# First modulations from re-laid pages of w_ada with FFN products between them, weight pages requested ahead in a fixed order, and position tables added to the latents by accumulating transfers

## The chip, the cores and the metric

The kernel runs on one core of a Trainium2 chip. Its engines are TensorE (PE in the profile: matmuls; PEld is its weight load), VectorE (DVE), ScalarE (ACT), GpSimd (POOL) and SyncE (SP, whose queue issues most of the DMA transfers). The metric is the device time of one execution in microseconds (us). The kernel's time is the median of several runs.

## The reference

One layer of a backbone over 1024 latent tokens `x` and 256 context tokens `ctx`, with 1024 channels in fp32. What the change touches is its beginning:

```python
h = x + grid_pos_emb(rows)          # sin/cos of the row: channels 0-511; of the column: 512-1023
hc = ctx
mods   = split(silu(c) @ w_ada + b_ada, 9)       # w_ada: 1024 x 9216; nine vectors of 1024
mods_c = split(silu(c_ctx) @ w_ada + b_ada, 9)

def ffn_sublayer(h, shift, scale, gate, g, w_in, w_out):     # D_FF = 2816
    hn = rmsnorm(h, g) * (1 + scale) + shift
    a, b = split(hn @ w_in, 2)
    return h + 0.5 * gate * ((silu(a) * b) @ w_out)

h  = ffn_sublayer(h,  mods[0],   mods[1],   mods[2],   ...)
hc = ffn_sublayer(hc, mods_c[0], mods_c[1], mods_c[2], ...)
...   # projections, mLSTM, spatial gating, output projection, second FFN on the latents, final norm
```

## The kernel before, in words

Channels lie on the 128 partitions, in eight tiles `d`. The context is `hc[d]` (128 x 256), the latents are `h[tb][d]` (128 x 512) for two halves `tb` of the tokens. All products are made of three fp32r matmuls, since each operand is split into a high and a low part: `split` (L145, L146) writes the high part on ACT (a cast) and the low part on DVE (a subtraction).

**The head.** The first FFN on the context needs the modulations 0 (shift) and 1 (scale) for silu(c_ctx); the latents need the same two for silu(c) somewhat later. The first 2048 columns of `w_ada` (8.4 MB) are loaded in four quarters of two channel tiles each, 32 transfers of 256 KB with rows of 1 KB (`ada_page`, L845). For quarters 0, 1 and 3 PE multiplies two columns (silu(c), silu(c_ctx)) with the pages, 512 columns at a time, and gets rows (`ada_rows`, L851), which are copied out (`ada_copy`) and turned into columns by small matmuls (`ada_flip`). Quarter 2 is accumulated on DVE (`side`, L794) and reduced. `ada_done` and `ada_side` add the bias into `mods` and make `smod`; `mod0` then makes the modulated context `hnc[d]` as high and low part, two tiles at a time. `idle(n)` puts filler matmuls on PE (`junk`, L923). The order of PE, DVE and ACT up to the end of hidden feature tile f=0 is written out by hand (`manual_schedule`); behind it a scheduler sets each engine's order.

**The first product of the context's FFN.** `W` (`Weights`) streams 44 weight pages W0 to W43 of 512 KB, two for each of 22 feature tiles f. Each has a raw page (`raw`, loaded at L126) and a split page (`hl`, 3 buffers); a page is asked for when a split page may be taken, and SP's queue holds the requests in that order. `proj` (L182) makes 24 matmuls of 256 columns per page. Results go through ACT and DVE to `gc` and to DRAM (`gcsp`).

**The latents beside it.** At f = 1 to 8 the loop asks for the two tiles of `xT` of one channel tile (256 KB each). At f = 2 to 9 it queues, for the gaps of DVE and ACT, the position add (`add_pos`, L917, from a table `pos` of 128 x 320 in SBUF, 160 KB) and the square and sum of the norm (`Norm.sq`, L210). At f = 10 come the norm's sums on PE (`Norm.rstd`, L215), the broadcast (L231) and the normalisation in place. After the 44 pages PE goes on with the first product of the latents (`Stage`, L412).

**The output product of the latents' first FFN** (L536) runs through passes p of 11 weight pages each; `rw` are loads of w1o, `graw` of the gated features. In its second pass `base` reloads the latents from `xT` and adds the positions again (`add_pos` with a second copy of the table, `pos2`), since the residual is added there.

Of the kernel before, what the change touches and what calls it, by code (L numbers as in the profile page):

```python
# [23 lines left out]
NKT = D // 128  # L24
# [31 lines left out]
def _build(ctx, tc, nc, a, out):  # L56
# [50 lines left out]
    class Weights:  # L107


        def __init__(self, order, name):  # L110
            self.c = ExitStack()
            self.pool = self.c.enter_context(tc.tile_pool(name=name, bufs=1, reuse_waits="tile"))
            self.order = deque(order)
            self.ready = deque()
            self.held = 0
            self.n = 0

        def load(self):
            n, i, w = self.order.popleft()
            src = a[n][i]  # L120
            if self.n % 4 < 2:
                raw = self.pool.tile([128, w], F32, name="raw", tag="raw", bufs=2)
            else:
                raw = hnp.tile([128, w], F32, name="raw", tag="pg0" if self.n == 2 else "pg1", bufs=8)
            self.n += 1
            nc.sync.dma_start(raw, src)  # L126
# [12 lines left out]
        def done(self, n=1):  # L139
            self.held -= n  # L140
            while self.order and self.held < 3:
                self.load()
# [635 lines left out]
    cp.tile([128, 32], F32, name="pad")  # L778

    def ada_load(page, m, hf, k):  # L780
        pgt = page()
        o = m * 1024 + hf * 512
# [53 lines left out]
    NQ = 4  # L836
    QW = 1024 // NQ
    QD = QW // 128
    KP = 512 // QW

    def ada_page(qt, kp, tag):
        pg = hnp.tile([128, KP, 2, QW], F32, name="adapg", tag=tag, bufs=8)
        for i in range(KP):
            src = a["w_ada"][kp * KP + i].rearrange("p (m c) -> p m c", m=9)[:, 0:2, qt * QW:(qt + 1) * QW]
            nc.sync.dma_start(pg[:, i], src)  # L845
        return [pg[:, i].rearrange("p m c -> p (m c)") for i in range(KP)]

    def ada_rows(pr, pgs, kp):
        for i, pg in enumerate(pgs):
            k = kp * KP + i  # L850
            T.matmul(pr[0:2, 0:2 * QW], sc2[:, :, k], pg, start=k == 0, stop=k == NKT - 1, skip_group_check=True)  # L851

    def ada_copy(pr):
        row = t2("adrow", shape=(2, 2 * QW))
        S.copy(row, pr[0:2, 0:2 * QW])
        return row

    def ada_flip(pc, row):
        for j in range(2 * QD):
            T.matmul(pc[:, 2 * j:2 * j + 2], row[:, j * 128:(j + 1) * 128], ident[0:2, 0:2], start=True, stop=True,  # L860
                     skip_group_check=True)

    def ada_side(qt, reds):
        bv = vs_("b_ada").rearrange("p (m d) -> p m d", m=9)
        cs = slice(qt * QD, (qt + 1) * QD)
        p8 = sm_ps("p8")
        for q, red in enumerate(reds):
            T.matmul(p8[:, q * 16:q * 16 + 16], grp4, red[:, 0:16], start=True, stop=True)
        for q in (1, 0):
            for r in range(4):  # L870
                sl = slice(32 * r, 32 * r + 32)
                V.tensor_add(mods[sl, 0:2, q, cs],
                             p8[sl, q * 16:q * 16 + 16].rearrange("p (m d r) -> p m d r", m=2, r=4)[:, :, :, r], bv[sl, 0:2, cs])
            scale_mod(0, 1, q, "g_ffn1", cs)

    def ada_done(qt, pc):
        sl = slice(qt * QD, (qt + 1) * QD)
        bv = vs_("b_ada").rearrange("p (m d) -> p m d", m=9)
        for q in (1, 0):
            V.tensor_add(mods[:, 0:2, q, sl],  # L880
                         pc[:, 0:4 * QD].rearrange("p (m d q) -> p m d q", m=2, q=2)[:, :, :, q], bv[:, 0:2, sl])
            done = scale_mod(0, 1, q, "g_ffn1", sl)
        return done
# [20 lines left out]
    pos = fxpage("pos", F32, (128, 320))  # L904

    def load_c(hcp, n):
        for i, pg in enumerate(hcp):
            nc.sync.dma_start(pg, a["cT"][i * n:(i + 1) * n].rearrange("d p t -> p d t"))

    def add_pos(tb, d, h=h, pos=pos):  # L910
        hv = h[tb][d].rearrange("p (r c) -> p r c", c=64)
        if d < 4:
            pv = pos[:, d * 16 + tb * 8:d * 16 + tb * 8 + 8].unsqueeze(2).to_broadcast([128, 8, 64])
        else:
            o = 64 + (d - 4) * 64
            pv = pos[:, o:o + 64].unsqueeze(1).to_broadcast([128, 8, 64])
        V.tensor_tensor(hv, hv, pv, ALU.add)  # L917
# [11 lines left out]
    def mod0(*ds):  # L929
        ts = [t2("nt")[:, 0:256] for _ in ds]  # L930
        for d, t in zip(ds, ts):
            S.activation(t, hc[d], AF.Identity, bias=mods[:, 0, 1, d:d + 1], scale=smod[:, 0, 1, d:d + 1])
            S.copy(hnc[d][:, 0, :], t)
        for d, t in zip(ds, ts):
            (V if d % 2 else G).tensor_tensor(hnc[d][:, 1, :], t, hnc[d][:, 0, :].bitcast(F32), ALU.subtract)

    def scaled0():
        for d in range(NKT):
            V.tensor_tensor(hc[d], hc[d], nct.rb, ALU.mult)
# [3 lines left out]
    sides = [t2("adacc") for _ in range(2)]  # L943

    def side(kp, pgs):
        for i, pg in enumerate(pgs):
            for q in range(2):
                ada_acc(V, sides[q], pg, q, kp * KP + i, kp + i == 0)

    load_c(hcp, 4)  # L950
    pgs = {}
    for qt, kp in ((2, 0), (0, 0), (0, 1), (2, 1), (0, 2), (0, 3), (2, 2), (1, 0), (1, 1), (2, 3), (1, 2), (1, 3),
                   (3, 0), (3, 1), (3, 2), (3, 3)):
        pgs[qt, kp] = ada_page(qt, kp, "pg1" if qt % 2 else "pg0")
    idle(30)
    for d in range(NKT):
        nct.sq(d)
    side(0, pgs[2, 0])
    prs = {0: mm_ps("adr")}
    ada_rows(prs[0], pgs[0, 0], 0)  # L960
    nct.rstd()
    ada_rows(prs[0], pgs[0, 1], 1)
    idle(3)
    side(1, pgs[2, 1])
    ada_rows(prs[0], pgs[0, 2], 2)
    nct.bcast()
    ada_rows(prs[0], pgs[0, 3], 3)
    row = ada_copy(prs[0])
    scaled0()
    side(2, pgs[2, 2])  # L970
    idle(4)
    pc = sm_ps("adc")
    ada_flip(pc, row)
    ada_done(0, pc)
    mod0(0, 1)
    prs[1] = mm_ps("adr")
    for kp in range(NKT // KP):
        ada_rows(prs[1], pgs[1, kp], kp)
    row = ada_copy(prs[1])
    side(3, pgs[2, 3])  # L980
    reds = [cp.tile([128, 32], F32, name="adred", tag="adred", bufs=2) for _ in range(2)]
    for acc, red in zip(sides, reds):
        ada_red(acc, red, 0)
    prs[3] = mm_ps("adr")
    ada_rows(prs[3], pgs[3, 0], 0)
    pc = sm_ps("adc")
    ada_flip(pc, row)
    ada_done(1, pc)
    mod0(2, 3)
    ada_rows(prs[3], pgs[3, 1], 1)  # L990
    ada_side(2, reds)
    for kp in (2, 3):
        ada_rows(prs[3], pgs[3, kp], kp)
    W.load()
    mod0(4, 5)
    row = ada_copy(prs[3])
    W.load()

    def last0():
        pc = sm_ps("adc")  # L1000
        ada_flip(pc, row)
        ada_done(3, pc)
        mod0(6, 7)
        W.load()

    nc.sync.dma_start(pos, a["pos"])
# [10 lines left out]
    for f in range(NF):  # L1017
        if 0 < f <= NKT:
            for tb in range(2):
                nc.sync.dma_start(h[tb][f - 1], a["xT"][f - 1, :, tb * 512:(tb + 1) * 512])  # L1020
        if 2 <= f < 2 + NKT:
            for tb in range(2):
                slow(add_pos, tb, f - 2)
                slow(n1[tb].sq, f - 2)
# [9 lines left out]
        if f > 12:  # L1034
            A.preload()
        wa = W.take("w1i", 2 * f)
        wb = W.take("w1i", 2 * f + 1)
        if f % 2 == 0:
            pa, pb = mm_ps("pa"), mm_ps("pb")
        for ks in (range(6), (6, 7)) if f == 0 else (range(NKT),):  # L1040
            for pt, w_ in ((pa, wa), (pb, wb)):
                proj(pt[:, f % 2 * 256:f % 2 * 256 + 256], w_, hnc, f % 2 == 0 and ks[0] == 0, ks)
                if f == 0 and ks[0] == 0 and pt is pa:
                    last0()
                if ks[-1] == NKT - 1:
                    W.done()
        if f == 0:
            order.close()
# [88 lines left out]
    pos2 = A.rg.tile([128, 512], F32, name="ft", tag="ft", bufs=1)[:, 0:320]  # L1137
    nc.sync.dma_start(pos2, a["pos"])

    def base(hv, tb, d):  # L1140
        return (lambda: nc.sync.dma_start(hv[tb][d], a["xT"][d, :, tb * 512:(tb + 1) * 512]),
                lambda: add_pos(tb, d, hv, pos2))
# [13 lines left out]
    load_c(hcp, 2)  # L1156
# [1172 lines left out]
def layout(x, c, ctx, c_ctx, w_ada, b_ada, g_ffn1, w_ffn1_in, w_ffn1_out, g_mix, w_in, b_gates,  # L2329
# [15 lines left out]
    r["cT"] = np.ascontiguousarray(ctx.T).reshape(8, 128, 256)  # L2345
# [61 lines left out]
```

## Time and profile before

| what | value |
|---|---|
| runs | 2642.66, 2642.14, 2639.4 us, median 2642.14 us |
| profiled execution | 2639.9 us, of which the span of the instructions is 2638.1 us |
| granted TensorE clock, mean | 0.997 |
| busy | PE 99%, PEld 84%, DVE 75%, ACT 46%, POOL 3% of the span |
| transfers | 448.5 MB, mean 170 GB/s |
| chain that ended last | PE 93%, DVE 2%, issue 2%, DMA 2%, ACT 1% |

Busy is the time in which an engine has an instruction under way; for PE that includes fillers. The chain that ended last is followed back from the last instruction, at each step to what released it. The DMA figures are a mean over stages of very different load, so the stages have to be read one by one.

### The profile page before, as it was taken

Reading aid. Unit: us, or ns where it says so; the run is one execution under the profiler, and the core shown is the slowest. Engines: PE = TensorE matmul, PEld = TensorE weight load, DVE = VectorE, ACT = ScalarE, POOL = GpSimd, SP = SyncE. Lnnn points to the kernel's source line nnn. Section 1 sums busy time; section 2 is a strip of 40 time slices with the busy share of each in tenths; the row PEclk is TensorE's granted clock in tenths of the full one; section 3 lists DMA queues with packets and bytes.
Section 4 is the critical chain, followed back from the end, with each engine's and each line's share of the span. In section 5 each row is a group of like instructions: output and inputs, shape, how many; then the busy total and the mean of one; then the engine's idle time right before and its main releaser. Section 6 shows DMA issues by size and latency. Waiting matters only on the chain.

```text
span 2638.1 us, 35899 instructions
## 1 busy us (share of the span) xinstructions
PE 2621.8 (99%) x12856; PEld 2205.1 (84%) x12856; DVE 1978.8 (75%) x3546; ACT 1205.6 (46%) x2175; POOL 75.8 (3%) x158
## 2 busy tenths in 40 slices
PE   9999999999999999999999999999999999999998
PEld 6998888888889878888888888888887888888887
DVE  7988688687989646777765878778799766665855
ACT  5664344444347525564443454333346444344433
POOL 0000000000000000000000002221000000000000
PEclk9999999999999999999999999999999999999999
DMA  9833344368587222346653566546341333337644
GB/s 312 311 113 127 128 164 161 117 224 307 169 283 268 77 80 85 111 162 205 196 172 112 166 206 247 180 150 206 125 157 39 128 136 123 113 125 282 199 159 177
DMA packets 200083, 448.54 MB, mean 170 GB/s; under 512 B 20192, under 2 KB 54496, under 8 KB 199904
## 3 DMA queue, kind: packets, MB, share of 16 engines
q1 hardware_dynamic: 199472, 445.85, 49.6%
q8 instruction: 101, 1.65, 0.3%
q14 instruction: 78, 0.64, 0.1%
q10 hardware_dynamic: 432, 0.39, 0.0%
HBM read 324.92 MB, written 121.32 MB: 169 GB/s over the span
## 4 chain that ended last, share of the span: by engine, by line
PE 93%; DVE 2%; issue 2%; DMA 2%; ACT 1%; SPq 0%; POOL 0%; POOLq 0%; ACTq 0%; DVEq 0%
PE qa L412 18%; PE pq L1380 17%; PE po L536 13%; PE qb L412 13%; PE pt L1864 6%; PE pr L1299 6%; PE po L2239 3%; PE pa L182 2%; PE pc L1166 2%; PE pb L182 2%; PE pn L2024 2%; PE pu L1700 1%; PE pn L2022 1%; PE pkc L1359 1%; PE pvc L1456 1%
## 5 line engine op out<-in xcount | busy, mean ns | idle before, releaser
L146 DVE TENSOR_TENSOR ring<-rawq,ring 128x512 fp32r<-128x512 f32 x408 | 281.3, 690 | 221.2 <-ACT ring L145 218.5
L536 PE MATMUL po<-gring,wring 128*128 128x512 f32 (+1 forms) x1896 | 424.0, 384 | 0.1
L536 PEld LDWEIGHTS po<-gring,wring 128*128 128x128 f32 x1896 | 349.4, 188 | 70.8 <-ACT px L693 0.9
L145 ACT CAST ring<-rawq 128x512 fp32r<-128x512 f32 x408 | 253.4, 622 | 309.2 <-PE pq L1380 86.1
L412 PE MATMUL qa<-fc,ring 128*128 128x512 f32 x1056 | 252.3, 389 | 0.0
L412 PEld LDWEIGHTS qa<-fc,ring 128*128 128x128 f32 x1056 | 198.2, 188 | 41.4 <-DVE fc L146 0.4
L1380 PE MATMUL pq<-fc,ring 128*128 128x512 f32 x864 | 207.3, 392 | 0.0
L145 ACT CAST wring<-rw 128x512 fp32r<-128x512 f32 x154 | 95.7, 622 | 216.6 <-PE po L536 184.7
L1380 PEld LDWEIGHTS pq<-fc,ring 128*128 128x128 f32 x864 | 161.4, 188 | 33.0
L1864 PE MATMUL pt<-yp,ring 128*128 128x512 f32 x768 | 184.4, 394 | 0.0
L1864 PEld LDWEIGHTS pt<-yp,ring 128*128 128x128 f32 x768 | 143.0, 188 | 28.2
L146 DVE TENSOR_TENSOR wring<-rw,wring 128x512 fp32r<-128x512 f32 x154 | 105.6, 686 | 80.7 <-ACT wring L145 80.5
L1380 PE MATMUL pq<-fa,ring 128*128 128x512 f32 x576 | 141.9, 394 | 0.0
L1380 PE MATMUL pq<-fb,ring 128*128 128x512 f32 x576 | 136.8, 391 | 0.0
L412 PE MATMUL qa<-fa,ring 128*128 128x512 f32 x528 | 129.6, 395 | 3.5 <-DVE ring L146 3.5
L412 PE MATMUL qa<-fb,ring 128*128 128x512 f32 x528 | 126.8, 390 | 0.0
L412 PE MATMUL qb<-fb,ring 128*128 128x512 f32 x528 | 126.6, 389 | 0.0
L1380 PEld LDWEIGHTS pq<-fb,ring 128*128 128x128 f32 x576 | 107.5, 188 | 22.4 <-issue 0.2
L412 PE MATMUL qb<-fc,ring 128*128 128x512 f32 x528 | 126.2, 389 | 0.0
L412 PE MATMUL qb<-fa,ring 128*128 128x512 f32 x528 | 126.2, 389 | 0.0
L1380 PEld LDWEIGHTS pq<-fa,ring 128*128 128x128 f32 x576 | 106.9, 188 | 21.9 <-DVE ring L146 0.2
L794 DVE SCALAR_TENSOR_TENSOR adacc<-adapg,sc,adacc 128x512 f32<-128x512 f32 x154 | 111.8, 747 | 17.8 <-DMA adapg<-in_w_ada_dram 17.0
(380 smaller groups left out, 4671.5 us busy)
## 6 DMA issues: line engine op xcount, KB each, us to landing
adapg<-in_w_ada_dram SPq DMA_DIRECT2D x144, 256.0 KB, 3.7
fsp<-fhl SPq DMA_DIRECT2D x66, 512.0 KB, 2.7
gring<-fsp SPq DMA_DIRECT2D x66, 512.0 KB, 4.3
raw<-in_w1i_dram SPq DMA_DIRECT2D x44, 512.0 KB, 5.4
graw<-fsp SPq DMA_DIRECT2D x88, 256.0 KB, 3.2
rawq<-in_w1i_dram SPq DMA_DIRECT2D x38, 512.0 KB, 3.7
rawq<-in_w2i_dram SPq DMA_DIRECT2D x38, 512.0 KB, 3.4
fsp<-p SPq DMA_DIRECT2D x66, 256.0 KB, 2.1
```

The costliest lines, as they stand in the source:

```text
L145: hi = S.copy(hl[:, 0, :], src)
L146: return hi, V.tensor_sub(hl[:, 1, :], src, hl[:, 0, :].bitcast(F32))
L182: T.matmul(pt, x, y, start=first and i == 0, stop=i == n - 1, skip_group_check=True)
L412: T.matmul(pt, hl[:, x, sl], pages[p][k][:, y, :], start=first and i == 0, stop=i == 11, skip_group_check=not first)
L536: T.matmul(pt[:, cs], w[:, x, sl], g[:, y, cs], start=grp and kp == 0 and i == 0, stop=kp == NFP - 1 and i == 2, skip_group_check=not grp)
L794: eng.scalar_tensor_tensor(acc, pgt, sc2[:, q, k:k + 1], acc, ALU.mult, ALU.add)
L1166: T.matmul(pt, hl[d // 4][:, x, sl], g[:, y, :], start=f == 0 and d % 2 == 0 and i == 0, stop=f == NF - 1 and i == 2, skip_group_check=True)
L1299: T.matmul(self.pt[m], pg[:, x, sl], hl[:, y, :], start=first and k == 0 and i == 0, stop=k == 3 and i == 2, skip_group_check=not first)
L1380: T.matmul(pt, hl[:, x, k * 128:(k + 1) * 128], pg[k][:, y, :], start=first and k == 0 and i == 0, stop=k == 3 and i == 2, skip_group_chec ...
L1864: T.matmul(pt, hl[:, x, k * 128:(k + 1) * 128], pg[:, y, :], start=kh + k + i == 0, stop=kh == 1 and k == 3 and i == 2)
L2024: T.matmul(pn[:, 0:257], qi[:, c_, :], self.C[d][:, c_, :], start=False, stop=c_ == 1)
L2239: T.matmul(pt, hl[:, x, k * 128:(k + 1) * 128], FO[p][k][:, y, :], start=first and k == 0 and i == 0, stop=k == 3 and i == 2, skip_group_c ...
```

## The change

1. `w_ada`'s first 2048 columns are re-laid on the host into 16 units (m, d) of 512 KB, each one channel tile d of modulation m, with rows of 4 KB. Eleven units (`UNITS`) are used as stationary operand on PE, 8 fp32 matmuls each (L949), and give columns for both conditioning vectors at once. Five units (`SIDE`), transposed, go to DVE: one fused multiply and reduction per conditioning vector against the vector spread over all partitions (`scB`). `spread` makes that on PE for the context; the latents' one is a broadcast load. The latents' five reductions are queued at f = 2 to 6.
2. The matmuls of f=0 and f=1 (`first`) stand between the units, channel tile by channel tile, as `mod0` delivers them. Order by hand now ends behind f=1. Fillers: 16 instead of 30 + 3 + 4.
3. Units, context halves and weight pages are requested in one written order. `W` fetches raw pages as soon as a raw buffer is to be had, up to eight ahead of the split, with five split pages instead of three; requests for `xT` and for the next stage are kept behind the last weight page asked for (`issue_after`).
4. `add_pos` no longer runs on DVE: the tables are expanded on the host to `posx` (8 x 128 x 1024), and a transfer on the GpSimd queue adds 256 KB from DRAM to each latent tile, 16 in the first product's stage and 16 in the output product's. The two loads of the small table go.

```diff
 class Weights:
-        def load(self):
+        def fetch(self):
             n, i, w = self.order.popleft()
             src = a[n][i]
             if self.n % 4 < 2:
                 raw = self.pool.tile([128, w], F32, name="raw", tag="raw", bufs=2)
             else:
-                raw = hnp.tile([128, w], F32, name="raw", tag="pg0" if self.n == 2 else "pg1", bufs=8)
+                raw = hnp.tile([128, w], F32, name="raw", tag="pg1", bufs=8)
             self.n += 1
-            nc.sync.dma_start(raw, src)
-            hl = self.pool.tile([128, 2, w], F32R, name="hl", tag="hl", bufs=3)
+            with ExitStack() as es:
+                if self.asked is not None:
+                    es.enter_context(tc.issue_after(self.asked.ins))
+                self.asked = nc.sync.dma_start(raw, src)
+            self.raws.append((n, i, w, raw))
+
+        def load(self):
+            if not self.raws:
+                self.fetch()
+            n, i, w, raw = self.raws.popleft()
+            hl = self.pool.tile([128, 2, w], F32R, name="hl", tag="hl", bufs=5)
             split(hl, raw)
             self.ready.append((n, i, hl))
             self.held += 1
+            if self.order:
+                self.fetch()
...
-    def add_pos(tb, d, h=h, pos=pos):
...
-        V.tensor_tensor(hv, hv, pv, ALU.add)
+    def add_pos(tb, d, h=h):
+        G.dma_start(h[tb][d], a["posx"][d, :, tb * 512:(tb + 1) * 512], accum_op=ALU.add)
...
+    for u in ("hc0", (1, 0), "hc1", (1, 1), (0, 0), (1, 2), (0, 1), (1, 3), (0, 2), "W", (0, 3), (1, 4), "W", (0, 4), (1, 5),
+              (0, 5), "W", (1, 6), (0, 6), "W", (1, 7), (0, 7), "W", "W", "W", "W"):
+        if u == "W":
+            W.fetch()
+        elif u in ("hc0", "hc1"):
+            load_c(hcp, 4, int(u[2]))
+        else:
+            fetch_unit(*u)
...
+    def side(m, d, q):
+        V.tensor_tensor_reduce(waste, page[m, d], scB[q], 1.0, vs_("b_ada")[:, m * 8 + d:m * 8 + d + 1], ALU.mult, ALU.add,
+                               mods[:, m, q, d:d + 1])
...
+    def unit(m, d):
...
+        for k in range(NKT):
+            T.matmul(pc[:, c:c + 128].rearrange("p (r q) -> p r q", q=2), page[m, d][:, k * 128:(k + 1) * 128],
+                     sc2[:, :, k].unsqueeze(1).to_broadcast([128, 64, 2]), start=k == 0, stop=k == NKT - 1,
+                     skip_group_check=True)
...
-    for f in range(NF):
-        if 0 < f <= NKT:
+    for f in range(1, NF):
+        if f <= NKT:
+            with tc.issue_after(W.asked.ins):
+                for tb in range(2):
+                    nc.sync.dma_start(h[tb][f - 1], a["xT"][f - 1, :, tb * 512:(tb + 1) * 512])
             for tb in range(2):
-                nc.sync.dma_start(h[tb][f - 1], a["xT"][f - 1, :, tb * 512:(tb + 1) * 512])
+                add_pos(tb, f - 1)
         if 2 <= f < 2 + NKT:
+            if f - 2 < len(SIDE):
+                slow(side, *SIDE[f - 2], 0)
             for tb in range(2):
-                slow(add_pos, tb, f - 2)
                 slow(n1[tb].sq, f - 2)
```

PE's order in the head before, from the last row products to the second weight page (`adr`, `p8`, `adc`: modulations; `pa`, `pb`: products of f=0; the number behind a name is the tile's own):

```order
L851 MATMUL adr_347<-adapg_181,sc2_98 2x512 x2
L868 MATMUL p8_369<-adred_339,cst_86 128x16
L868 MATMUL p8_369<-adred_340,cst_86 128x16
L851 MATMUL adr_347<-adapg_184,sc2_98 2x512 x2
L851 MATMUL adr_347<-adapg_187,sc2_98 2x512 x2
L182 MATMUL pa_408<-hnc_132,hl_388 128x256 x6
L182 MATMUL pa_408<-hnc_133,hl_388 128x256 x6
L182 MATMUL pa_408<-hnc_134,hl_388 128x256 x6
L860 MATMUL adc_428<-cst_86,adrow_399 128x2 x4
L182 MATMUL pb_409<-hnc_132,hl_403 128x256 x6
```

And now, from the eighth unit to the ninth and tenth (L949 with `adaU` is a unit, L195 is the line of `proj`):

```order
L949 MATMUL adc_354<-sc2_98,adaU_161 128x128 x8
L195 MATMUL pa_372<-hnc_131,hl_309 128x256 x6
L949 MATMUL adc_380<-sc2_98,adaU_167 128x128 x8
L195 MATMUL pa_372<-hnc_132,hl_309 128x256 x3
L195 MATMUL pb_373<-hnc_131,hl_349 128x256 x6
L195 MATMUL pb_373<-hnc_132,hl_349 128x256 x3
L949 MATMUL adc_413<-sc2_98,adaU_173 128x128 x8
L195 MATMUL pa_372<-hnc_132,hl_309 128x256 x3
```

The products moved in front of the last units; behind the last of the eleven (`adaU_179`) 60 matmuls of f=0 and f=1 are left.

SP's queue before, where the last pair of latent tiles is asked for (`raw` is a weight page, `raw_985` W18, `h` a latent tile; the waits are on semaphores of earlier transfers and on engines):

```order
L126 DMA raw_952<-in_w1i_dram 128x1024 [waits DMAHW1_49,DVE_49]
L1064 DMA gcsp_105<-gc_846 128x512 [waits DMAHW2_49,Activation_49]
L1064 DMA gcsp_105<-gc_847 128x512 [waits DMAHW3_49,DVE_49]
L126 DMA raw_985<-in_w1i_dram 128x1024 [waits DMAHW4_49,PE_49]
L1020 DMA h_119<-in_xT_dram 128x512 [waits DMAHW5_49]
L1020 DMA h_127<-in_xT_dram 128x512 [waits DMAHW6_49]
L126 DMA raw_1031<-in_w1i_dram 128x1024 [waits DMAHW7_49]
```

And now the same place (`raw_999` is W28, `raw_970` W27):

```order
L131 DMA raw_970<-in_w1i_dram 128x1024 [waits DMAHW6_49]
L1121 DMA gcsp_105<-gc_1004 128x512 [waits DMAHW7_49,Activation_49]
L131 DMA raw_999<-in_w1i_dram 128x1024 [waits DMAHW0_49,DVE_49]
L1121 DMA gcsp_105<-gc_1005 128x512 [waits DMAHW1_49,DVE_49]
L1078 DMA h_119<-in_xT_dram 128x512 [waits DMAHW2_49]
L1078 DMA h_127<-in_xT_dram 128x512 [waits DMAHW3_49]
L131 DMA raw_1049<-in_w1i_dram 128x1024 [waits DMAHW4_49,DVE_49]
```

The last pair stood behind W18 and now stands behind W28; the first two pairs stand behind W16. W28's raw buffer was W24's, which DVE must have split, into the split page that PE's use of W19 makes free.

PE's order at the latents' norm sums before (`p4`; `pa_1144` and `pb_1145` are f=10, whose pages are W20 and W21):

```order
L182 MATMUL pb_1002<-hnc_135,hl_1033 128x256 x6
L182 MATMUL pa_1144<-hnc_132,hl_1066 128x256 x6
L215 MATMUL p4_1152<-ones_88,acc_583 128x1 x4
L182 MATMUL pa_1144<-hnc_133,hl_1066 128x256 x6
L182 MATMUL pa_1144<-hnc_134,hl_1066 128x256 x6
L215 MATMUL p4_1193<-ones_88,acc_615 128x1 x4
L182 MATMUL pa_1144<-hnc_135,hl_1066 128x256 x6
```

And now (`pb_1154` ends f=11 with page W23; `pa_1358` is f=12):

```order
L195 MATMUL pb_1154<-hnc_133,hl_1110 128x256 x6
L195 MATMUL pb_1154<-hnc_134,hl_1110 128x256 x6
L228 MATMUL p4_1161<-ones_88,acc_591 128x1 x4
L195 MATMUL pa_1358<-hnc_131,hl_1139 128x256 x4
L228 MATMUL p4_1202<-ones_88,acc_610 128x1 x4
L195 MATMUL pa_1358<-hnc_131,hl_1139 128x256 x2
```

The sums moved from the start of f=10 (16 pages behind the end of f=1) to the start of f=12 (20 pages).

More of the change, by code (lines that the diff above doesn't have):

```diff
@@ L834, in ada_steps @@
             yield
[L836 to L883, printed above, removed]
+    SIDE = ((0, 0), (0, 4), (0, 5), (0, 6), (0, 7))
+    UNITS = ((1, 0), (1, 1), (1, 2), (0, 1), (1, 3), (0, 2), (0, 3), (1, 4), (1, 5), (1, 6), (1, 7))
+    BANK = {0: 0, 1: 0, 2: 1, 3: 1, 4: 2, 5: 3, 6: 4, 7: 5}
     smod = cp.tile([128, 3, 2, 8], F32, name="smod")
@@ L950, in _build @@
[L950 to L960, printed above, removed]
+    V.tensor_scalar(bias1, vs_("b_ada")[:, 8:16], 1.0, None, ALU.add)
+    idle(16)
@@ L961, in _build @@
+    unit(1, 1)
+    side(0, 0, 1)
+    unit_done(1, 0)
     nct.rstd()
[L962 to L965, printed above, removed]
+    unit(1, 2)
+    unit(0, 1)
     nct.bcast()
[L967 to L978, printed above, removed]
```

233 lines of the change are left out of this document (160 added, 73 removed).

## Prediction

> **What bounds the kernel now.** I read the page's table of engines first, then the chain of waits of the first 60 us, then the windows and the DMA view of the stages that the diff touches.
>
> ```profile
> PE 2621.8 (99%) x12856; PEld 2205.1 (84%) x12856; DVE 1978.8 (75%) x3546; ACT 1205.6 (46%) x2175; POOL 75.8 (3%) x158
> ```
>
> TensorE (PE) is busy in 99% of the span, but a busy PE is not always PE at useful work. In the head the chain of waits shows what it does:
>
> ```profile
> 0.99 9.07 PE junk L923 x60
> 36.09 1.24 DVE hl L146
> 37.38 2.18 PE pa L182 x16
> ...
> 45.67 2.64 PE pa L182 x22
> 48.31 2.64 PE pb L182 x22
> 50.95 2.88 PE pa L182 x24
> ```
>
> Columns: start, length, what. PE starts with 30 filler matmuls (60 records, 9.07 us) and begins the first FFN product at about 37 us. Hidden features f=0 and f=1 are done at 50.95; I call this point T0. From there a weight page is 24 matmuls in 2.88 us (0.12 us each), one after the other. What the head waits for is the load:
>
> ```profile
> GB/s 0 163 231 377 352 348 352 348 348 349 349 348 349 356 335 350 348 349 349 348 391 394 399 408 150 98 324 408 382 307 359 232 180 213 315 255 363 262 310 359
> adapg<-in_w_ada_dram SPq DMA_DIRECT2D x32, 256.0 KB, 6.1
> h<-in_xT_dram SPq DMA_DIRECT2D x9, 256.0 KB, 5.5
> ```
>
> This is the DMA view of 0 to 60 us, in slices of 1.5 us. The 32 loads of w_ada (8.4 MB, rows of 1 KB) run at 348 GB/s; the W pages behind them (30 to 36 us, rows of 4 KB) at 391 to 408.
>
> After T0 both the transfers and PE are close to full. Three windows, one row of the timeline, SP's waits of 0 to 170 us, and the rows of the position adds:
>
> ```profile
> 60.00:70.00 10.00, 10.00 (x86) 10.00 (x85) 8.86 (x12) 6.95 (x10) 0.00 (x0) 1.00 0.93 320
> 90.00:100.00 10.00, 10.00 (x87) 10.00 (x85) 7.55 (x12) 5.59 (x8) 0.00 (x0) 1.00 0.96 317
> 106.00:168.00 62.00, 62.00 (x516) 61.83 (x515) 59.38 (x81) 47.22 (x69) 0.00 (x0) 1.00 0.59 208
> 97.59 0.95 PE L215 MATMUL p<-ones,acc 128*128 128x1 f32 x8
> SPq L126 <- DVE hl L146: 55.6, 20, 6.4
> L917 DVE TENSOR_TENSOR h<-h,pos x16: 682/685/695, 43.4 to 85.4; 128x512 f32<-128x512 f32 x16
> L917 DVE TENSOR_TENSOR h<-h,ft x16: 682/685/694, 620.9 to 654.4; 128x512 f32<-128x512 f32 x16
> ```
>
> The windows give PE, PEld, DVE, ACT and POOL busy time, granted clock, DMA share and GB/s. DMA is 93 to 96% busy up to the latents' norm sums on PE (row of 97.59); after them VectorE (DVE) is, 59.38 of 62. SP's queue waits 55.6 us in the first 170 for splits of weights (L126 behind DVE), so a transfer queued behind a weight page goes out late. The two L917 rows are the 32 position adds.
>
> The adds' second stage is the FFN's output product near 620 us. Windows, then the DMA view of 620 to 640, a row of the chain and two of the timeline:
>
> ```profile
> 610.00:620.00 10.00, 10.00 (x46) 8.07 (x46) 6.30 (x16) 6.21 (x12) 0.00 (x0) 1.00 0.98 324
> 620.00:630.00 10.00, 9.86 (x43) 7.79 (x42) 6.36 (x10) 3.72 (x7) 0.00 (x0) 1.00 0.98 356
> 630.00:640.00 10.00, 10.00 (x45) 8.28 (x45) 7.07 (x11) 4.64 (x8) 0.00 (x0) 1.00 1.00 370
> DMA packets 3076, 7.27 MB, mean 363 GB/s; under 512 B 340, under 2 KB 340, under 8 KB 3075
> q1 hardware_dynamic: 3075, 7.25, 98.3%
> rw<-in_w1o_dram SPq DMA_DIRECT2D x6, 512.0 KB, 6.3
> h<-in_xT_dram SPq DMA_DIRECT2D x9, 256.0 KB, 6.3
> 609.55 7.56 DMA rw<-in_w1o_dram
> 588.51 1.75 PE L536 MATMUL po<-gring,wring 128*128 128x512 f32 x7
> 637.64 0.69 DVE L146 TENSOR_TENSOR wring<-rw,wring 128x512 fp32r<-128x512 f32 x1 [0.50 <-ACT wring L145]
> ```
>
> The transfers stand at 98 to 100%, and the chain already runs through a load of w1o at 609.55. Of the second pass, page 8's split is done at 637.64+0.69 = 638.3. PE started the product at 588.51 and takes 12 matmuls of about 10/44 us, 2.72 us, per page; the window of 620 lacks two or three of them (0.5 us). Page 8, after 11 pages of the first pass and 8 of the second, is due at 588.5+19x2.72+0.5 = 640.7. The slack is 2.4 us.
>
> **The change part by part.**
>
> Head. Out go 21 of 37 fillers, the row products, their copies, flips and DVE reductions; in come 8 spreading matmuls, 11 units of 8 matmuls on PE and five reductions on DVE. A row with 128x128 fp32 matmuls only, two records each:
>
> ```profile
> 6.00:8.00 2.00, 2.00 (x20) 2.00 (x19) 1.19 (x3) 1.86 (x7) 0.00 (x0) 1.00 1.05 346
> ```
>
> That is 0.2 us a matmul, so 1.6 us a unit. On PE: fillers to about 6 us, spreading 1.6, units 17.6, norm and broadcast about 1.5, then 60 products of 0.12 us behind the last unit: 34 us, earlier than the loads allow. The loads up to the last unit are 0.1 (vec), 0.13 (cst), 1.05 (hc), 8.4 (16 units) and 2.1 MB (four W pages): 11.8 MB. All have rows of 4 KB now, except small ones, so I take the rate of the W pages, about 400 GB/s: 29.5 us from about 2 us, plus 2 for the tail of a landing, 33.7. Then one unit (1.6) and 60 x 0.12 = 7.2: T0 = 42.5, a gain of 8.5. At 348 GB/s the load ends 4.4 us later and the gain is about 4; if the last transfers overlap more it is 9.5. I take 8.5, since the rows of 4 KB are the nearest.
>
> Position adds in the FFN's first product. Off DVE go 16 x 0.685 = 11 us, worth nothing here: PE ends every step to 97 us, and the five extra reductions for the latents (about 1.2 each by the row of 128x1024 below) come in. In come 16 transfers of 256 KB on the GpSimd queue, each behind its xT load. POOL is idle in the windows above, so nothing queues behind them there but each other. They land on the DMA. On PE, the norm sums now stand 20 pages behind T0 (the order rows above), 20 x 2.88 = 57.6; before, 16 pages. By then the DMA must bring W9 to W28 (20 pages, 10.5 MB; the five split pages and the raw buffers hold those up to W8), xT (4.2), 8 gcsp (2.1) and the added pages (4.2): 21.0 MB in 57.6 us, 365 GB/s. The rows above had 317 to 320 at a share of 0.93 to 0.96, and the best full stretch 363. There is no slack.
>
> Latency bounds it from below. The last xT pair stands behind W28 on SP, whose buffer is free when PE is done with W19 (16 pages after W3: T0+46.1) and W24 is split. A cast, the groups of splits and of sums on DVE, and the page's row of w_ada's loads:
>
> ```profile
> 44.06 1.06 ACT hl L145
> L146 DVE TENSOR_TENSOR hl<-raw,hl 128x1024 fp32r<-128x1024 f32 x38 | 46.4, 1220 | 3.6 <-ACT hl L145 3.5
> L210 DVE TENSOR_TENSOR acc<-acc,sq 128x512 f32<-128x512 f32 x14 | 9.0, 683 | 0.0
> adapg<-in_w_ada_dram SPq DMA_DIRECT2D x144, 256.0 KB, 3.7
> ```
>
> T0+46.1+1.06+1.22 = T0+48.4; xT 5.5; the adding transfer, if it is like a load, 5.5; square and sum about 1.4: T0+60.8, so PE stalls 3.2. With the quiet 3.7 for both: T0+57.2, no stall. From above: an addition in SBUF must read what it adds to. If each added byte costs two, 25.2 MB at 363 GB/s take 69.4 us, and with 1.4 behind it the stall is 13.2. I take the middle of 3.2 and 13.2, 8.2, for want of any row of such a transfer. The Trainium skill, "Collectives: The Full Stack", section "The bandwidth ceiling: the fold count and why AG ≠ RS ≠ AR", says that a reducing transfer emits two read descriptors for a chunk where a copy emits one, and that reads are its limit: 62.28 against 32.35 GB/s measured there. By it the sum would take the upper ends here and below, +16.7 in all; no run here shows such a transfer so far.
>
> A stalled PE also loses clock:
>
> ```profile
> 1970.00:1980.00 10.00, 10.00 (x46) 8.28 (x45) 9.80 (x16) 8.70 (x15) 0.00 (x0) 1.00 0.44 157
> 1980.00:1990.00 10.00, 6.50 (x27) 5.08 (x26) 9.82 (x17) 6.84 (x12) 0.00 (x0) 0.93 0.45 159
> 1990.00:2000.00 10.00, 10.00 (x37) 8.04 (x37) 7.14 (x19) 3.58 (x9) 0.00 (x0) 0.73 0.00 1
> ```
>
> After 3.5 us idle the granted clock was 0.73; 28 of 92 matmuls are missing, 6.4 us for 3.5 idle, so 2.9 more. I take 2.9 for a stall of 8, half of it for one of 3.
>
> Behind the sums DVE has the latents' normalisation: 59.38 of 62 busy before. The sums come 11.5 us later after T0, but splits run five pages ahead instead of three, and the last pages' splits are done sooner. I count these as equal: 0, with up to 2 lost.
>
> The stage at 620 us. Out go 16 adds (11 us of DVE, not the bound: 6.36 and 7.07 of 10 busy) and the 160 KB load of the table; in come 16 transfers of 256 KB into a DMA that is 98 to 100% busy. About ten xT loads stand ahead of the last w1o page, so about eight adding transfers fall before it lands. At 0.262/0.363 = 0.72 us each that is 5.8, less the slack of 2.4: 3.4 lost. If each costs two: 9.1. Below nothing is excluded, since nothing leaves the DMA there but one table. I take the middle, 6.2.
>
> Raw pages fetched up to eight ahead cost nothing by themselves: SP's order puts xT behind them, which the latency above holds.
>
> Sum: -8.5+8.2+2.9+6.2 = +8.8 on 2639.9, the profiled execution (span 2638.1), so about 2648. The median of the three runs shown, 2642.1, is 2.2 above it, and they differ by 3.3; 0.2% is 5.3 us, about what a measurement can tell from no change.
>
> **The rivals.**
>
> An adding transfer costs as much as a load, no more. For it: what is read from DRAM and written to SBUF is the same as for xT, and no row shows that the reading of a destination takes a share. Against it: the read of the old value. -8.5+3.2+1.5+3.4 = -0.4: 2639, no change.
>
> The adding transfers are hidden (the other side: faster). Both places decide it: the last addition lands within 3.7 us of its xT, and w1o still lands with 2.4 to spare because additions wait for their xT loads and slip behind it. For it: the 144 loads of w_ada over the whole kernel take 3.7 us in the median, and total demand of 365 GB/s is close to the row's 363. Against it: latencies in these two stages are 5.5 and 6.3. The time is that of the head alone, 2631. From a landing of 3.7 on, each further microsecond of the pair costs one.
>
> Each addition costs two loads, in full. -8.5+13.2+2.9+9.1 = +16.7: 2656. For it: the old value has to be read, and neither stage has slack. The page of the Trainium skill named above gives the same time. Against it: a stall of 13 us ends the queueing, and w1o pages that stand in line on other queues may pass the additions.
>
> The head doesn't gain. If the 1 KB rows were not the reason for 348 GB/s, the gain is 4 instead of 8.5, and my forecast becomes 2653; this lies in its range.
>
> **How the numbers follow.** Contention at a price between one load and two: 0.36, 2648 (its own range 2640 to 2656). Two loads in full: 0.12, 2656. One load: 0.27, 2639. Hidden: 0.25, 2631. The range goes from 2630 to 2659: it leaves out a part of the hidden case (0.05), the upper part of the dear one (0.05) and of the forecast's with a slow head (0.05). Faster by over 0.2% (below 2637): most of the hidden case and some of the one-load case, 0.30. Slower (above 2647): the dear case, half to two thirds of the forecast, a little of one load, 0.39. Within: 0.31. The bounds of these three stand around the median of the runs shown, 2642.
>
> **What would show it.** Head: the last of 11 units on PE at about 34 to 35 us, and the product of f=2 at 42 to 43 instead of 50.95. First place: the norm sums at T0+57.6 plus a stall with a DMA as releaser, and a granted clock below 0.9 in the window behind it; DMA share near 1.0 from T0 to there. No idle PE at the sums speaks for the hidden case, about 3 us for one load, 13 for two; the time from issue to landing of the adding transfers beside that of xT says which. Second place: PE idle between 635 and 650 until splits of w1o. I would be wrong in the sign if those two are empty of idle time, or if the head ends past 46.

## The result, and the profile after

The changed kernel takes 2682.8 us in the median (2680.3 to 2687.2), the kernel before 2642.4 us: the ratio is 1.0158, with a 95% interval of 1.0146 to 1.0170. It is 40.4 us slower, where 8.8 were forecast.

The page of the changed kernel: the table of engines and the chain that ended last.

```profile
PE 2631.9 (98%) x12930; PEld 2227.5 (83%) x12930; DVE 1958.4 (73%) x3497; ACT 1203.6 (45%) x2170; POOL 104.6 (4%) x190
PE 88%; DMA 5%; DVE 3%; issue 2%; ACT 1%; POOL 0%; SPq 0%; POOLq 0%; DVEq 0%; ACTq 0%
```

Before, 93% of the chain was PE and 2% DMA. Now 5% is DMA, some 130 us, and the chain says where. Its rows around the start of f=2 come first:

```profile
41.47 1.08 PE pb L195 x9
42.55 2.88 PE pa L195 x24
...
95.82 0.57 ACT sil L1110
96.40 0.95 ACT hl L158
97.37 1.22 DVE hl L159
98.60 0.61 DVE gc L1119
99.23 0.65 SPq L1121
...
99.92 5.23 DMA h<-in_xT_dram
...
106.46 9.03 DMA h<-in_posx_dram
...
116.05 0.58 ACT sil L1110
```

The head does what it was built for: T0 is 42.55 instead of 50.95. Behind it one turn of a loop stands in the chain. The silu of a context result on ACT (`sil`, 95.82) lets DVE finish `gc`; SP then stores it (L1121) and only after that asks for the next latent tiles (5.23 us); the adding transfer follows (9.03 us); ACT takes its square; and behind the square stands the next silu, 20.2 us after the last one. PE consumes the two features of a turn in 4 x 2.88 = 11.5 us. The windows show the beat (columns as in the prediction: busy us of PE, PEld, DVE, ACT and POOL, granted clock, DMA share, GB/s):

```profile
60.00:70.00 10.00, 5.58 (x47) 5.38 (x45) 2.45 (x2) 2.63 (x3) 3.65 (x4) 0.91 1.03 324
70.00:80.00 10.00, 3.66 (x17) 3.66 (x18) 4.41 (x6) 4.46 (x7) 1.72 (x2) 0.50 0.86 164
80.00:90.00 10.00, 10.00 (x79) 10.00 (x79) 4.28 (x4) 3.68 (x4) 1.77 (x2) 0.91 0.81 239
90.00:100.00 10.00, 4.04 (x21) 3.83 (x20) 4.07 (x6) 3.86 (x6) 1.73 (x2) 0.77 0.85 200
```

Where these windows had 85 to 87 matmuls before, there are 47, 17, 79 and 21. PE idles 4.4 to 6.3 us in three of the four, and the granted clock falls to 0.50 behind the idle time. The waits of 45 to 150 us (total us, times, longest) say for what, and three rows of ACT's timeline show the order that makes it:

```profile
PE pa L195 <- ACT sil L1110: 22.6, 3, 10.8
ACT sq L222 <- DMA h<-in_posx_dram: 18.9, 8, 5.0
PE p L228 <- DVE acc L223: 3.8, 1, 3.8
```

```profile
93.31 0.63 ACT L222 ACTIVATE sq<-h 128x512 f32<-128x512 f32 x1 [4.57 <-DMA h<-in_posx_dram]
95.28 0.63 ACT L222 ACTIVATE sq<-h 128x512 f32<-128x512 f32 x1 [1.34 <-DMA raw<-in_w1i_dram]
95.82 0.58 ACT L1110 ACTIVATE sil<-pa 128x512 f32<-128x512 f32 x1
```

PE waits 22.6 us for silus, which free the banks that its next products go into, and only 3.8 for the norm sums. ACT does not wait for anything of the silu's own: it waits for an adding transfer, for the square that stands in front of the silu. The order of the program has it so (`h_115` and `h_123` are the latent tiles of d=3, on the DMASW semaphores of the adding transfers). It also shows that the 1.34 us of the second square, which the profile puts down to a weight page, are no weight page's: that square waits for its own adding transfer (DMASW7) and for an earlier store of gc (DMAHW4):

```
L222 ACTIVATE sq_807<-h_115 128x512 [waits DMASW6_49]
L222 ACTIVATE sq_827<-h_123 128x512 [waits DMAHW4_49,DMASW7_49]
L1110 ACTIVATE sil_853<-pa_717 128x512 [waits DMAHW0_49]
L158 CAST hl_996<-raw_702 128x1024 [waits DMAHW4_49,PE_49,Activation_49]
L1118 CAST gc_856<-sil_853 128x512 [waits DVE_49]
```

The second place, beside the output product. Windows, the DMA view of 650 to 700 us and the group of the product:

```profile
660.00:670.00 10.00, 10.00 (x46) 8.29 (x45) 3.37 (x5) 3.00 (x5) 2.62 (x3) 1.00 1.07 343
670.00:680.00 10.00, 7.82 (x31) 4.99 (x29) 2.07 (x3) 1.86 (x3) 2.18 (x3) 1.00 1.07 324
680.00:690.00 10.00, 7.44 (x27) 5.99 (x27) 6.70 (x11) 4.04 (x7) 3.07 (x4) 0.83 1.10 307
```

```profile
q1 hardware_dynamic: 5315, 11.27, 62.3%
q0 software_dynamic: 2229, 4.07, 45.2%
h<-in_xT_dram SPq DMA_DIRECT2D x13, 256.0 KB, 10.9
rw<-in_w1o_dram SPq DMA_DIRECT2D x5, 512.0 KB, 11.4
```

```profile
L549 PE MATMUL po<-gring,wring 128*128 128x512 f32 (+1 forms) x1896 | 428.0, 386 | 7.2 <-ACT wring L158 4.7 <-DMA gring<-fsp 2.1 <-DVE gring L159 0.2
```

The DMA is over 100% busy for 50 us, yet moves less than the 356 and 370 GB/s of before. The 4.07 MB of q0, the adding transfers, take 45.2% of the engines' time, the 11.27 MB of q1 62.3%: 11.1% per MB against 5.5%. A page of w1o lands 11.4 us after its issue instead of 6.3, and PE waits for its split: 4.7 us for `wring`, 7.2 in all, where it waited 0.1 before.

To tell the two places apart I take, in each profile, the time from T0 to the first matmul of `po`, and from there to the first of `pc` (the context's output product). A stage's change is against the kernel before, whose figures are 537.6 and 212.5. The starts of `po` and `pc` are read to 0.1 us, so a change is good to about that.

| run | median us | T0 | first stage | second stage |
|---|---|---|---|---|
| before | 2642.4 | 50.95 | 537.6 | 212.5 |
| changed | 2682.8 | 42.55 | +38.9 | +11.1 |
| adds on DVE in both places | 2640.3 | 42.28 | +3.2 | -0.6 |
| adds on DVE in the second place | 2671.5 | 42.42 | +39.1 | -0.6 |
| plain transfers | 2665.7 | 42.33 | +28.7 | +1.4 |
| gc stores on ACT's queue | 2686.8 | 42.07 | +36.9 | +9.7 |
| xT ahead from W7 | 2659.1 | 50.65 | +7.8 | +9.1 |
| squares four features later | 2656.3 | 42.18 | +11.4 | +10.5 |
| before, with adding transfers | 2661.1 | 50.91 | +9.1 | +10.6 |
| DVE adds, xT ahead from W7 | 2637.6 | 41.98 | +2.4 | -0.6 |
| DVE adds, xT ahead from W9, table early | 2634.0 | 42.08 | +0.1 | -0.6 |
| xT ahead from W10 | 2668.4 | 42.68 | +21.3 | +10.5 |
| the same, plain transfers | 2647.7 | 42.69 | +14.8 | +2.3 |

For the changed kernel -8.4+38.9+11.1 = 41.6, near the 40.4 of the medians. The table is from one profiled execution each, which stands up to 7 us off the median of its runs. A later stage that no edit touches varies by as much: from the first to the last of the mLSTM's `pn` matmuls it takes 231 to 237 us in these thirteen profiles, 232.0 in the one before and 236.3 in the changed one, and why is not known. One of the nine executions of the last row's kernel took 4399 us at a granted clock of 0.56; without it the median would be 0.2 us lower.

### The profile page after: what moved, and what is told of

It is laid out like the page before. It is cut to its first block, busy times and chain, and to the rows that moved or that the text cites. A ratio compares the mean times of both kernels' runs of the same rounds, so it can differ in the third digit from the quotient of the medians.

```text
span 2685.4 us, 36060 instructions
## 1 busy us (share of the span) xinstructions
PE 2631.9 (98%) x12930; PEld 2227.5 (83%) x12930; DVE 1958.4 (73%) x3497; ACT 1203.6 (45%) x2170; POOL 104.6 (4%) x190
## 4 chain that ended last, share of the span: by engine, by line
PE 88%; DMA 5%; DVE 3%; issue 2%; ACT 1%; POOL 0%; SPq 0%; POOLq 0%; DVEq 0%; ACTq 0%
PE qa L425 18%; PE pq L1437 17%; PE qb L425 13%; PE po L549 12%; PE pt L1921 6%; PE pr L1356 6%; PE po L2296 3%; PE pc L1223 2%; PE pn L2081 2%; PE pu L1757 1%; PE pa L195 1%; DMA h<-in_posx_dram 1%; PE pkc L1416 1%; PE pb L195 1%; PE pn L2079 1%
## 5 line engine op out<-in xcount | busy, mean ns | idle before, releaser
L425 PEld LDWEIGHTS qa<-fa,ring 128*128 128x128 f32 x528 | 101.2, 193 | 26.1 <-DVE ring L159 4.7
```

Source lines behind the costliest of these rows:

```text
L425: T.matmul(pt, hl[:, x, sl], pages[p][k][:, y, :], start=first and i == 0, stop=i == 11, skip_group_check=not first)
```

## The experiments

**The adds back on DVE, in both places.**

```diff
-            for tb in range(2):
-                add_pos(tb, f - 1)                    # adding transfer
...
             for tb in range(2):
+                slow(add_pos_v, tb, f - 2, h, pos)    # VectorE, table of 128 x 320
                 slow(n1[tb].sq, f - 2)
```

> All 32 position adds are back on VectorE from the small table; the new head, the five split pages and the order of requests stay. Loop theory (ScalarE's squares wait for adding transfers that take 8 to 10 us, the silu and the casts stand behind them in ScalarE's order, the stores of gc behind those in SP's, and the next xT loads behind the stores, so that a turn of two features lasts 20 us instead of 11.5): the 9 us of the transfer leave the turn, no stall is left, 2633 (2630 to 2640). Double-read theory (the DMA is simply too full): 2632 as well. Order theory (xT asked for behind W16 to W28 is too late, whoever adds): at least half of the first stage's 39 us stays, 2650 or more.

Measured: 2640.3 us, ratio 0.9996 (0.9987 to 1.0006). All but 3 us of both stages' loss is gone, so the adding transfers are needed for it. But the time is that of before, not 2633. Of 8.7 us gained in the head, 3.2 go again in the first stage. The last pair of xT still stands behind W28, and PE idles around the norm sums (chain, and a window, 1.7 us idle):

```profile
93.71 6.59 DMA h<-in_xT_dram
...
101.67 1.05 PE p L228 x8
```

```profile
100.00:110.00 10.00, 8.33 (x69) 8.24 (x69) 8.08 (x29) 3.91 (x7) 0.00 (x0) 1.00 0.55 190
```

That leaves some 5 us between the stages' figures and the median: the profiled execution, 2636.1, was the fastest of ten, and where the others lose them no profile shows. The varying stage of `pn` is one candidate.

**The adds on DVE in the second place alone.** The edit is the same in `base` only.

> Only the second 16 adds, beside the output product, are back on VectorE; the first 16 stay adding transfers. If the two places add up, as the trace says (first stage +39.5 against before, second +11), 2672 (2668 to 2676): the first stage as in the changed kernel, the second as before. If the second stage's loss is one of the other edits (order, missing table load), it stays near 2682.

Measured: 2671.5 us, ratio 1.0116 (1.0101 to 1.0131). The second stage is as before (-0.6), the first as in the changed kernel (+39.1): the places add up, and the second one's loss is the adding transfers'.

**Plain transfers in place of adding ones.**

```diff
-        G.dma_start(h[tb][d], a["posx"][d, :, tb * 512:(tb + 1) * 512], accum_op=ALU.add)
+        G.dma_start(h[tb][d], a["posx"][d, :, tb * 512:(tb + 1) * 512])
```

> The 32 transfers of the position pages overwrite the latents instead of adding to them (so the position pages take the place of the latents): same queue, same bytes from DRAM, same waits, only the addition is left out. Double-read theory: the transfer lands in about 5.5 us instead of 8 to 9, and the DMA is less full; second stage down from +11 to +3, first stage from 39 to about 10: 2640 to 2650. Loop theory: a turn of 20 us loses some 3.5 us, so the first stage still stalls about 20 to 25: 2655 to 2665. If the latency is that of the GpSimd queue and not of the addition: no change, 2680 or more.

Measured: 2665.7 us, ratio 1.0092 (1.0076 to 1.0107): the upper end of what the loop gives. The DMA view of 60 to 135 us, of the changed kernel first and then of this one:

```profile
q0 software_dynamic: 2304, 4.20, 33.9%
h<-in_posx_dram POOLq DMA_DIRECT2D x16, 256.0 KB, 7.9
```

```profile
q0 software_dynamic: 1280, 4.20, 16.4%
h<-in_posx_dram POOLq DMA_DIRECT2D x16, 256.0 KB, 5.9
```

The same 4.20 MB take 33.9% of the engines' time when added and 16.4% when copied, a factor of 2.07, and land in 7.9 instead of 5.9 us. The second stage's loss falls from 11.1 to 1.4: there the addition is nearly all of it. The first stage's falls only from 38.9 to 28.7, since a turn of the loop is shorter by one or two us, 18.1 and 19.2 from silu to silu in this run's chain, but still longer than 11.5. PE waits 16.9 us for silus here.

**The stores of gc on ACT's queue.**

```diff
-            nc.sync.dma_start(gcsp[f // 2, y].rearrange("p f c -> p (f c)"), g[y].bitcast(F32))
+            nc.scalar.dma_start(gcsp[f // 2, y].rearrange("p f c -> p (f c)"), g[y].bitcast(F32))
```

> The stores of gc to DRAM (gcsp) go out from ScalarE's queue instead of SP's; all adding transfers stay. Loop theory: the xT loads no longer stand behind stores that wait for a silu that waits for the position transfers, so the loop is open; the first stage gets back at least half of its stall, 2652 to 2667. Double-read theory: the bytes are the same, 2682 within 4.

Measured: 2686.8 us, ratio 1.0172 (1.0157 to 1.0187). My loop theory, as I had put it, missed here: it promised 15 to 30 us. The group of PE's products from 36 to 200 us in this run:

```profile
L195 PE MATMUL pa<-hnc,hl 128*128 128x256 f32 x504 | 74.0, 306 | 24.9 <-ACT sil L1110 24.9
```

PE waits for silus as long as ever. That is not the cost of the stores on ACT, where squares wait only 1.6 us behind them for DVE's gc. The chain shows why: with the stores gone, xT still stands in SP's queue behind weight pages, whose raw buffers come free only when a cast on ACT and the split on DVE are done, and the casts stand behind the same squares.

```profile
93.72 0.94 ACT hl L158
94.69 1.24 DVE hl L159
96.71 4.49 DMA h<-in_xT_dram
...
102.50 8.35 DMA h<-in_posx_dram
```

So the loop closes over any request of SP that waits for ACT, and taking one of the two ways out leaves the other. The next two runs open it at other points.

**The xT loads earlier in SP's queue**, one pair ahead of each second weight page from W7 on:

```diff
+    def latents():                          # called ahead of each weight page's request
+        d, r = divmod(W.n - 7, 2)
+        if r == 0 and 0 <= d < NKT:
+            with tc.issue_after(W.asked.ins):
+                for tb in range(2):
+                    W.asked = nc.sync.dma_start(h[tb][d], a["xT"][d, :, tb * 512:(tb + 1) * 512])
+            for tb in range(2):
+                add_pos(tb, d)
```

> All 32 adding transfers stay, with the same bytes; only the place of the xT loads in SP's queue changes: one pair ahead of each second weight page from W7 to W21, where the changed kernel has them behind W16 to W28. Loop theory, widened after the run with the gc stores elsewhere (what closes the loop is any request of SP that waits for work behind ScalarE's squares: the weight pages' splits as much as the stores): squares find their tiles earlier than ScalarE comes to them, the loop stays open, first stage down from +39 to between 0 and +15: 2645 to 2660. If the stall is only the fullness of the DMA: the bytes are the same, 2675 or more.

Measured: 2659.1 us, ratio 1.0068 (1.0053 to 1.0083). With the same bytes PE no longer waits for silus. From 60 to 90 us the DMA share is 1.05 to 1.07 and PE is busy throughout at a clock of 1.00, so the full DMA did not by itself stall it. What PE waits for now:

```profile
L198 PE MATMUL pa<-hnc,hl 128*128 128x256 f32 x504 | 69.3, 291 | 8.1 <-POOL hnc L908 6.9 <-DVE hl L162 0.8 <-ACT hl L161 0.5
```

The 6.9 us are new and lie in the head: GpSimd's last subtraction of `mod0` stands behind adding transfers that wait for xT, so T0 is 50.65, and the gain of the head is gone. The first stage loses 7.8 from there. PE also starts this stage 8 us later here, which leaves the transfers more time; how much of the gain that makes is not told apart.

**The squares four features later**, at f = 6 to 13:

```diff
-        if 2 <= f < 2 + NKT:
...
+        if 6 <= f < 6 + NKT:
             for tb in range(2):
-                slow(n1[tb].sq, f - 2)
+                slow(n1[tb].sq, f - 6)
```

> All adding transfers and SP's order stay; the squares are queued four features later (f = 6 to 13 instead of 2 to 9), so that ScalarE comes to them when the transfers have landed; PE's norm sums move from f=12 to f=15 or 16. Loop theory: the silu and the casts no longer wait, the stalls at the silu go; what is left is that VectorE needs some 62 us from the sums to the gate and has 40 to 45, so 17 to 25 of the 39 stay: 2660 to 2668. Fullness theory: the stalls before the sums stay where they are and the late sums come on top: 2690 or more.

Measured: 2656.3 us, ratio 1.0058 (1.0043 to 1.0073), some us better than expected. All bytes and the places of the xT loads among the weight pages are those of the changed kernel; only some stores of gc moved in SP's queue, by a page or so, and the run with the stores on ACT's queue showed that their place gains nothing:

```profile
L195 PE MATMUL pa<-hnc,hl 128*128 128x256 f32 x504 | 67.3, 287 | 0.8 <-DVE hl L159 0.8
L228 PE MATMUL p<-ones,acc 128*128 128x1 f32 x16 | 3.2, 324 | 5.7 <-DVE acc L223 5.7
```

The 22.6 us for silus are gone, though ACT still waits 20.6 us for adding transfers in front of squares, and though the DMA moves more from 45 to 135 us (28.05 MB instead of 22.24) and an xT load lands after 9.7 us instead of 5.2. What was changed is the place of the squares on ACT, with DVE's sums and PE's norm sums behind them (these now at f=14). So the silus' place behind the squares is shown to be the cause of PE's waits for them. What is left, 11.4, lies at the late sums, in DVE behind them and in a clock of 0.80 and 0.86 there.

**The kernel before, with adding transfers and nothing else.**

> The kernel before, with one part of the change alone: the 32 adding transfers. Head, three split pages and the order of requests (xT from behind W4 to behind W18) are those of before. Second stage +11 in any case. Loop theory: the squares again stand ahead of silu and casts and wait 8 us for the transfer, but the loads go out earlier than in the changed kernel; first stage +10 to +25, 2663 to 2678. If the order of requests of the changed kernel is needed for the stall, only the doubled bytes count: first stage +0 to +8, 2653 to 2661.

Measured: 2661.1 us, ratio 1.0075 (1.0060 to 1.0090), between the two expectations: first stage +9.1, second +10.6. In this order of requests ACT waits for the transfers as long as in the changed kernel:

```profile
ACT sq L209 <- DMA h<-in_posx_dram: 19.6, 8, 5.3
PE pa L182 <- ACT hl L145: 4.5, 2, 3.8
```

but PE only 4.5 us for ACT, probably since xT is asked for earlier, behind W4 to W18. The 39 us of the changed kernel are thus neither the adding transfers' alone (9) nor those of the rest of the change alone (3, the first of these runs), but of both together.

**DVE adds with xT from W7, and the version that came of it.**

> No adding transfer at all (VectorE adds in both places), new head, and the xT loads early as in the first of these runs. If 3.6 us of the head's gain were lost between f=2 and the gate because the last pair of xT went out behind W28, they come back: 2635 (2631 to 2639). If they were lost to VectorE, which is full behind the norm sums: 2640, as with the later loads.

Measured: 2637.6 us, ratio 0.9985 (0.9975 to 0.9994). The norm sums no longer stall; but the first DVE add waits 5.2 us for its table, which stood behind W7, and PE 2.2 for a split behind that add. The last version asks for the table ahead of W4 and for xT from W9:

```diff
+    nc.sync.dma_start(pos, a["pos"])
     nc.sync.dma_start(scB[0], scq.rearrange("p k -> (p k)").partition_broadcast(128))
```

> VectorE adds in both places, new head, xT pairs ahead of each second weight page from W9, and the small position table asked for ahead of the pages behind W7 (in the run before, the first VectorE add waited 5.2 us for it and PE about 2.2). If that wait cost PE what it idled, 2.2 us come back: 2635 (2632 to 2638). If VectorE, 59 of 60 us busy behind the sums, sets the gate's start in any case: no change, 2637.6 within 1.

Measured: 2634.0 us, ratio 0.9971 (0.9962 to 0.9980): 8 us faster than the kernel before, nearly the whole gain of the head (8.9). Its chain is PE alone from f=2 to W43, the last weight page, behind which the latents' first product begins (the expectations call it the gate):

```profile
42.08 2.88 PE pa L198 x24
...
157.49 2.88 PE pb L198 x24
```

**Adding transfers with xT from W10**, so that none stands ahead of GpSimd's subtraction:

> All adding transfers; xT pairs ahead of each second weight page from W10 to W24, so that no adding transfer stands ahead of GpSimd's last subtraction of the head, on which PE waited 6.9 us in the run with xT from W7. Loop theory: that head stall goes, the rest stays open as there: 2652 (2648 to 2656). If each page later in SP's queue closes the loop again: 2660 to 2670. Fullness alone: as with W7, 2659.

Measured: 2668.4 us, ratio 1.0098 (1.0084 to 1.0112). The wait in the head is gone, as expected, and yet the run is 9 us slower than with W7 (8 when each is taken against the runs of the kernel before that were made with it), the second of the three expectations:

```profile
L198 PE MATMUL pa<-hnc,hl 128*128 128x256 f32 x504 | 69.7, 293 | 4.4 <-ACT sil L1118 4.0 <-DVE hl L162 0.3 <-POOL hnc L908 0.2
L231 PE MATMUL p<-ones,acc 128*128 128x1 f32 x16 | 3.6, 344 | 10.7 <-DVE acc L226 10.7
```

Silus are waited for again (4.0), and the sums, which the scheduler put at f=10 here, 10.7. ACT waits 25.0 us for adding transfers in front of squares. Three pages later in the queue, with PE 8 us further ahead, is enough for the transfers to come too late. How much of the 9 us is the queue's and how much PE's earlier start is not told apart.

**The same with plain transfers.**

> As the run with xT from W10, but the position pages overwrite the latents instead of adding (they take their place). Queues, waits and bytes from DRAM are the same; what goes is the reading of the old value. Double-read theory for what is left when the loop is open: first stage within 5 of before, second +1.4: 2638 (2634 to 2645). If the loop still holds, the plain transfer gains as little as it did in the late order: 2645 or more.

Measured: 2647.7 us, ratio 1.0022 (1.0012 to 1.0032), 20.6 us better than with additions but outside the 2634 to 2645 of the first theory.

```profile
L198 PE MATMUL pa<-hnc,hl 128*128 128x256 f32 x504 | 67.6, 288 | 0.0
L231 PE MATMUL p<-ones,acc 128*128 128x1 f32 x16 | 3.6, 344 | 10.2 <-DVE acc L226 10.2
```

No silu is waited for, so with a shorter transfer the loop is open here; the sums at f=10 still come 10.2 us too early for the chain of xT, transfer and square. Of the addition 8.2 us lie in the second stage (10.5 against 2.3) and 6.5 in the first, 14.7 in all. The 20.6 are of medians, and this run's profiled execution was 6.8 us above its median.

## Why the prediction was wrong

The sign and the places were right; the sum was too small by 32 us. One step carries most of that, some 28 us, and the second place another 5.

- **Head: right.** T0 was forecast at 42.5 from rows of 4 KB and 60 matmuls behind the last unit; it is 42.55, and the DMA ran at 408 to 410 GB/s from 10 to 30 us.
- **First place: the step that failed.** "T0+46.1+1.06+1.22 = T0+48.4 [...] so PE stalls 3.2": that step followed one chain, from the last xT to the norm sums, and named the sums as the only place where PE waits. The sums cost 3.8. What was queued behind the waiting squares on ACT was not asked: a silu, which frees PE's banks, and casts, on which SP's next requests hang, xT among them. The term was +8.2 and 2.9 for the clock; it is +38.9. The windows from 60 to 140 us show 26.5 us of idle PE, and some 9 lost to a clock of 0.50 to 0.91 (377 matmuls in 53.5 us of busy PE, where 680 took 80 before). That it was this, and not the fullness of the DMA, is shown by the squares queued later (same bytes, more of them moved by then, no wait for silus); the run with xT from W7, with a full DMA and no wait for silus, agrees. The forecast also took the DMA for 93 to 96% busy all the way to the sums; the two windows that it did not show, 70 to 90 us, have 84 and 88%.
- **The price of an addition: the middle was the wrong choice.** It is the upper end, two loads: 2.07 times the engines' time for the same bytes. The Trainium skill, "Collectives: The Full Stack", section "The bandwidth ceiling: the fold count and why AG ≠ RS ≠ AR", gives a measured ratio of 1.93 for rings between cores, where it names a second read as the reason. This case's 2.07 agrees for a transfer from DRAM into SBUF; that it is the reading of the old value, no run here shows. I had let the rule stand as a rival with 0.12, for want of a row of this kernel.
- **Second place: right in mechanism, too small.** PE waited for splits of w1o, as forecast; the slack of 2.4 us was not measured by itself. 6.2 was the middle of 3.4 and 9.1, and 11.1 was measured. The plain transfer costs 1.4 there where 3.4 was the estimate, so the addition itself makes 9.7.
- **The clock: right in kind.** A stalled PE lost clock: some 9 us, where 2.9 were put down for one dip; the stall came in four parts.
- **The rivals.** "Two loads in full" had the right price and the wrong sum, 2656, because it too had only one wait in the first stage. None had a queue behind a wait.

## What to carry to other kernels

When an operation on an in-order engine gets a new, slow input, list what stands behind it on that engine and follow each of those to who waits for it; if the list leads back to the request for that input, the latencies add up to the period of a loop, even where the DMA could carry more. An adding transfer is paid for twice on the DMA and its landing is 2 us longer, so it replaces a VectorE instruction of 0.7 us only where both the DMA and the waiting engine have room; here VectorE had it. A faster head is worth its whole gain only when what it feeds (here xT and a small table) moves ahead with it: of the same head came nothing that can be told from noise (0.8), 3 and 8 us, with three orders of requests.

## What had not been expected of the hardware

An adding transfer of 256 KB took twice the DMA time of a copy (33.9% against 16.4% of 16 engines over 75 us for 4.20 MB), in 2304 packets against 1280. Its issue holds GpSimd's queue 0.87 us, where SP's issues take about 0.33 (weight pages) to 0.43 (xT). A plain transfer on the same queue took 0.54. And the granted clock fell to 0.50 in a window of 10 us in which PE idled 6.3, after 4.4 in the one before; the kernel before showed 0.73 behind 3.5.
